# Turning the inverses of the scan's triangles with VectorE's 32x32 transpose and products with an identity instead of through DRAM

## The chip, the cores and the metric

The kernel runs on one core of one Trainium2 chip. The metric is the device time of one execution in microseconds. The kernel before took 2352.26 us, the median of three runs (2348.28 to 2355.29). Smaller is better.

## The reference

The kernel computes one layer of an encoder: a half-step feed-forward network, a mixing layer, a second half-step feed-forward network. Input and output are 1 x 1024 x 1024 float32 (1024 tokens, width 1024).

```python
x = x + 0.5 * post1(FFN1(pre1(x)))
h = pre2(x); z = h @ w_in        # attention q|k|v and RWKV-7 r|k|v|decay|iclr|gate
x = x + post2(concat(attn, rwkv) @ w_out)
x = x + 0.5 * post3(FFN2(pre3(x)))
```

The change touches the RWKV-7 group alone. It has 8 heads of 64 columns and runs over the tokens in both directions. For each direction and head it carries a 64 x 64 state from token to token:

```python
def _rwkv7_step(state, inp):
    r, w, k, v, kk, kka = inp
    sa = jnp.einsum('dbhvk,dbhk->dbhv', state, kk)
    state = state * w[..., None, :] - sa[..., :, None] * kka[..., None, :] + v[..., :, None] * k[..., None, :]
    y = jnp.einsum('dbhvk,dbhk->dbhv', state, r)
    return state, y
```

A token's `sa` needs the state that all tokens before it have left, so the sums inside a chunk of tokens form a system of linear equations with a unit lower triangular matrix, one matrix for each chunk, head and direction.

## The kernel before, in words

**The whole.** The two feed-forward networks (lines L81 and L415 for their products) take the start and the end of the span. Between them come the input projection, the attention, and from about 1180 to 1580 us the stage that this document is about: the scan, the RWKV-7 recurrence, with the output projection of the attention group mixed in as work that fills TensorE's waits.

**The scan.** The 1024 tokens of a direction are cut into 16 chunks of 64, and two chunks make a block, so there are 8 blocks. A chunk has 16 triangles (2 directions, 8 heads) of 64 x 64, a block 32. For each block four functions run:

- `prep(n)` loads the block's inputs (`th_w`, `th_a` and, in one load from `d_rk`, `in`), forms `pr` and `bk` on VectorE and ScalarE, multiplies them on TensorE into `lp` (L836, 32 products of a block), masks `lp` into the triangles `lm` on VectorE (L838), turns the other half of `bk` with `bp` (L844, a transposition through TensorE with an identity), and stores the two diagonal 32 x 32 blocks of every triangle to DRAM (`d_x`, L852).
- `solve(n)` inverts these 64 small triangles. It loads them as `X`, with one triangle on one partition (L862; each is loaded onto two partitions, one of which solves the left 16 columns of the inverse and the other the right 16), and runs 31 steps of forward substitution, two VectorE operations each (L872, L874), on `Ti`. At the end `Ti` has the inverses. VectorE copies a transposed version of them into the free part of `X` (L876). Both are written to DRAM, as `d_t` (L878) and `d_tt` (L879).
- `merge(n)` reads the inverses back from DRAM, now with rows on partitions, as `d` and `tt` (L889, L892), and puts the off-diagonal 32 x 32 block of every 64 x 64 inverse together: 32 products `pa` (L900), two copies by ScalarE (L902), 32 products `pb` (L906), two negations by ScalarE (L908). The result is `tt`, two buffers of which take turns.
- `chain(n)` runs the two chunks, and this is the sequential part. For each chunk: `xu` from the state `sv` (L947), a copy to `xs` by ScalarE (L950), `xu` again as `tt` times `xs` (L958), `uv` by ScalarE (L960), products `st` and `y` (L943), the next state `sv` by VectorE (L974). The values of `v` are loaded into `sv` and `uv` by `values` (L914).

**What sets the order.** The block program (L1262 to L1310) runs `prep` and `solve` of blocks 0 and 1 early, beside the input projection, then `merge(0)` and `prep`, `solve` of block 2, and then for each n: `merge(n)`, `chain(n)`, `prep` and `solve` of block n+3, and one or two tiles of the output projection (48 products `po` each, L1070, after `yat`, `yq`, `yah`, `yal`, whose weights `woh` and `wol` are made from `wor` by L1060). A scheduler decides each engine's order of instructions ahead of time, by priorities and its own estimate of when things are ready; on the chip each engine runs its list in that order and waits where something is not ready. The DMAs of L878, L879, L889, L892 and L914 are issued by GpSimd (POOL), the loads of `prep` and `solve` by SyncE (SP). `X`, `Ti` and their scratch `ttmp` have two buffers, `d` one, and the PSUM tile of `pa` and `pb` one.

Of the kernel before, what the change touches and what calls it, by code (L numbers as in the profile page):

```python
# [163 lines left out]
class _Kernel:  # L164
# [624 lines left out]
    def prep(self, n, p, psum, big):  # L789
# [59 lines left out]
        for par in range(2):  # L849
            for k in range(2):  # L850
                r0 = par * 64 + k * 32
                self.nc.sync.dma_start(_ap(self.x_d[n % 4], (k * 2 + par) * 16 * 1024, [[32, 32], [1024, 16], [1, 32]]),  # L852
                                  lm[r0:r0 + 32, par, :, :, :, k * 32:k * 32 + 32].rearrange("p d i a t -> p (d i a) t"))
        return blk

    def solve(self, n, p):


        nc, V, G = self.nc, self.nc.vector, self.nc.gpsimd
        X = p.tile([128, 32, 32], F32, name="X", tag="X", bufs=2)  # L860
        for q in range(2):
            self.load(X[q * 64:q * 64 + 64].rearrange("p a b -> p (a b)"), self.x_d[n % 4])  # L862
        Ti = p.tile([128, 32, 16], F32, name="Ti", tag="Ti", bufs=2)
        tmp = p.tile([128, 144], F32, name="ttmp", tag="ttmp", bufs=2)
        tf = Ti.rearrange("p a b -> p (a b)")
        G.memset(tf, 0.0)
        for q in range(2):
            G.memset(tf[q * 64:q * 64 + 64, q * 16:512:33], 1.0)
        for s in range(31):
            r, m = 31 - s, s // 2 + 1  # L870
            tv = tmp[:, :r * m].rearrange("p (a b) -> p a b", a=r)
            V.tensor_tensor(tv, X[:, s, s + 1:][:, :, None].to_broadcast([128, r, m]),  # L872
                            Ti[:, s, 0:m][:, None, :].to_broadcast([128, r, m]), op=OP.mult)
            V.tensor_tensor(Ti[:, s + 1:, 0:m], Ti[:, s + 1:, 0:m], tv, op=OP.subtract)  # L874
        Tt = X[:, 0:16, :]
        V.tensor_copy(Tt, Ti.rearrange("p a b -> p b a"))  # L876
        for q in range(2):
            self.nc.gpsimd.dma_start(_ap(self.t_d[n % 4], q * 16, [[1024, 32], [32, 32], [1, 16]]), Ti[q * 64:q * 64 + 32])  # L878
            self.nc.gpsimd.dma_start(_ap(self.tt_d[n % 4], q * 32, [[1024, 64], [64, 16], [1, 32]]), Tt[q * 64:q * 64 + 64])  # L879

    def merge(self, n, blk, p, psum):

        nc, A, T = self.nc, self.nc.scalar, self.nc.tensor
        NI, lm = 2 * BLK * 4, blk["lm"]
        d11 = p.tile([128, NI, 32], F32, name="d11", tag="d11")
        blk["tt"] = tt = self.tt[n % 2]
        for par in range(2):
            o = par * 64
            self.nc.gpsimd.dma_start(d11[o:o + 32], _ap(self.t_d[n % 4], par * 16 * 1024, [[32, 32], [1024, 16], [1, 32]]))  # L889
            for k in range(2):  # L890
                r0 = o + k * 32
                self.nc.gpsimd.dma_start(tt[r0:r0 + 32, :, k * 32:k * 32 + 32],  # L892
                          _ap(self.tt_d[n % 4], (k * 2 + par) * 16 * 1024, [[32, 32], [1024, 16], [1, 32]]))
        pa = psum.tile([128, NI, 32], F32, name="pa", tag="mg")
        am = d11
        lohi = [(slice(o, o + 32), slice(o + 32, o + 64)) for o in (0, 64)]
        for j in range(NI):
            d, i, pr = j // 8, j // 4 % 2, j % 4
            for par, (lo, hi) in enumerate(lohi):
                T.matmul(pa[hi, j, :], lm[lo, par, d, i, pr, 32:64], d11[lo, j, :], start=True, stop=True)  # L900
        for lo, hi in lohi:
            A.copy(am[hi].rearrange("p i (c q) -> p i q c", q=2), pa[hi].rearrange("p i (q c) -> p i q c", q=2))  # L902
        pb = psum.tile([128, NI, 32], F32, name="pb", tag="mg")
        for j in range(NI):
            for lo, hi in lohi:
                T.matmul(pb[lo, j, :], am[hi, j, :], tt[hi, j, 32:64], start=True, stop=True)  # L906
        for lo, hi in lohi:
            A.activation(tt[lo, :, 32:64], pb[lo], AF.Copy, scale=-1.0)  # L908

# [195 lines left out]
    def constants(self):  # L1105
# [6 lines left out]
        for c, t in self.eps.items():  # L1112
# [15 lines left out]
        self.y_d = [self.dram(f"y{d}", [4, 128, S]) for d in range(2)]  # L1128
        self.x_d, self.t_d, self.tt_d = ([self.dram(f"{n}{j}", [r, w]) for j in range(4)]
                                         for n, r, w in (("x", 64, 1024), ("t", 32, 1024), ("tt", 64, 1024)))  # L1130

# [37 lines left out]
    def run(self):  # L1169
# [5 lines left out]
        with self.top as top:  # L1175
# [98 lines left out]
            for n, ct in ((0, 8), (1, 10)):  # L1274
                blk[n] = self.prep(n, sp, pp, (R0, R1)[n])
                self.solve(n, sp)
                self.project_rwkv(zr, pz, x, [(ct, 1), (ct + 1, 1)])
# [13 lines left out]
            def upto(m):  # L1291
                while nxt[0] <= min(m, NB - 1):
                    n = nxt[0]
                    blk[n] = self.prep(n, sp, pp, (R0, R1, B0)[n % 3])
                    self.solve(n, sp)
                    nxt[0] += 1
# [145 lines left out]
```

## Time and profile before

| what | value |
|---|---|
| median of three runs | 2352.26 us (2348.28 to 2355.29) |
| the profiled execution's own time | 2347.61 us |
| its span in the profile | 2345.8 us (1.8 us lie around it) |
| mean granted TensorE clock | 0.962 |
| the scan | about 1180 to 1580 us of the span |
| first and last time that chunk 0 to 15 begin their second `xu` product (L958) | 1299.2 and 1564.3 us |

Times are positions in the span or durations in microseconds. A row of a group gives the line, the engine, the operation, output<-inputs, how many, then the busy time and the mean duration of one in ns, and behind the last bar how long the engine had been idle just ahead of them and who ended it. A row of the timeline gives the start, the length of a run of equal instructions, and in brackets the idle time ahead of it. A float32 product shows as two records on TensorE in these traces (`x64` are 32 products), a transposition through TensorE as one.

### The profile page before, as it was taken

To read this page: it belongs to the slowest core of one execution; us is meant where nothing else is said; L and a number is where in the kernel's file an instruction comes from. 1 tells how busy PE (TensorE), PEld (TensorE's weight loads), DVE (VectorE), ACT (ScalarE), POOL (GpSimd) and SP (SyncE) were. 2 spreads that over 40 slices of the span, in tenths; PEclk is the share of its full clock that TensorE was granted. 3 is DMA by queue.
4 is the path that set the end of the run, shared out by engine and by line. 5 is a ranking of instruction groups with operands and counts; after the bars stand their busy time and mean duration, and the time that the engine had idled before them with its cause. 6 is when DMAs were issued, how large, how long until landed. Compare 5 with 4: busy or idle time off the path is not lost. (4 is left out here: it accounts for less than half of the span.)

```text
span 2345.8 us, 39442 instructions
## 1 busy us (share of the span) xinstructions
PE 2198.8 (94%) x14532; PEld 1776.9 (76%) x14532; DVE 1761.8 (75%) x2869; ACT 1026.5 (44%) x1942; POOL 606.5 (26%) x740
## 2 busy tenths in 40 slices
PE   5999999999999998999996888988699999999997
PEld 4788888878877676788775777766578888887886
DVE  8899999965676244666668777737899999986565
ACT  4333232354567412666544645445443323235453
POOL 6244444410000010111112232332424444441000
PEclk8999999999999998999996898989899999999998
DMA  5344444476671514443269767587435444447665
GB/s 153 99 168 160 172 148 171 160 265 194 197 228 74 218 45 127 117 116 96 60 180 221 192 174 181 136 242 244 157 119 170 161 171 149 171 161 260 191 191 181
DMA packets 360084, 388.13 MB, mean 165 GB/s; under 512 B 74450, under 2 KB 265810, under 8 KB 359892
## 3 DMA queue, kind: packets, MB, share of 16 engines
q1 hardware_dynamic: 309216, 278.53, 39.6%
q0 software_dynamic: 30320, 94.44, 11.4%
q10 hardware_dynamic: 20356, 12.66, 1.8%
q8 instruction: 114, 1.87, 0.3%
q14 instruction: 78, 0.64, 0.1%
HBM read 259.63 MB, written 125.89 MB: 164 GB/s over the span
## 5 line engine op out<-in xcount | busy, mean ns | idle before, releaser
L186 ACT ACTIVATE wh<-raw 128x512 fp32r<-128x512 f32 (+1 forms) x273 | 168.4, 626 | 272.0 <-PE gu L81 96.0
L187 DVE TENSOR_TENSOR wl<-raw,wh 128x512 fp32r<-128x512 f32 (+1 forms) x273 | 275.8, 1013 | 4.1 <-ACT wh L186 3.3
L81 PE MATMUL gu<-xh,wh 128*128 128x512 f32 x704 | 276.9, 394 | 1.1 <-ACT xh L186 1.1
L81 PE MATMUL gu<-xl,wh 128*128 128x512 f32 x704 | 275.9, 392 | 0.0
L81 PE MATMUL gu<-xh,wl 128*128 128x512 f32 x704 | 275.4, 391 | 0.0
L415 PE MATMUL pd<-gl,gwh 128*128 128x512 f32 x616 | 241.2, 392 | 2.9 <-DVE gl L187 2.9
L415 PE MATMUL pd<-gh,gwh 128*128 128x512 f32 x616 | 240.2, 391 | 0.6 <-DVE row L86 0.6
L415 PE MATMUL pd<-gh,gwl 128*128 128x512 f32 x616 | 240.6, 391 | 0.0
L86 DVE TENSOR_TENSOR row<-gu,row 128x512 f32<-128x512 f32 x308 | 206.4, 682 | 25.6 <-PE gu L81 25.2
L187 DVE TENSOR_TENSOR gwl<-graw,gwh 128x512 fp32r<-128x512 f32 (+1 forms) x176 | 116.9, 667 | 127.9 <-ACT gwh L186 125.3
L116 POOL DMA_DIRECT2D d_hid<-row x154 | 84.7, 551 | 471.3 <-DVE row L114 449.2
L186 ACT ACTIVATE gwh<-graw 128x512 fp32r<-128x512 f32 (+1 forms) x176 | 101.4, 576 | 188.6 <-PE pd L415 157.9
L81 PEld LDWEIGHTS gu<-xh,wh 128*128 128x128 f32 x704 | 133.3, 190 | 30.1 <-ACT xh L186 2.8
L81 PEld LDWEIGHTS gu<-xl,wh 128*128 128x128 f32 x704 | 133.2, 189 | 27.5
L81 PEld LDWEIGHTS gu<-xh,wl 128*128 128x128 f32 x704 | 133.1, 189 | 27.6
L415 PEld LDWEIGHTS pd<-gl,gwh 128*128 128x128 f32 x616 | 116.0, 188 | 27.9 <-DVE gl L187 4.1
L415 PEld LDWEIGHTS pd<-gh,gwh 128*128 128x128 f32 x616 | 116.0, 188 | 25.6 <-DVE row L86 0.9
L415 PEld LDWEIGHTS pd<-gh,gwl 128*128 128x128 f32 x616 | 116.1, 188 | 24.1
L187 DVE TENSOR_TENSOR gl<-raw,gh 128x512 fp32r<-128x512 f32 x160 | 112.8, 716 | 18.4 <-ACT gh L186 18.2
L94 ACT ACTIVATE row<-row 128x512 f32<-128x512 f32 x44 | 27.7, 632 | 221.1 <-DVE row L86 213.6
L145 POOL TENSOR_TENSOR ws<-ws 128x512 f32<-128x512 f32 x88 | 114.3, 1299 | 1.2
L186 ACT ACTIVATE gh<-raw 128x512 fp32r<-128x512 f32 x160 | 98.1, 621 | 35.7 <-DMA raw<-in_ffn_w_down_dram 21.7
(351 smaller groups left out, 5292.1 us busy)
## 6 DMA issues: line engine op xcount, KB each, us to landing
d_hid<-row POOLq DMA_DIRECT2D x154, 256.0 KB, 2.4
graw<-d_hid SPq DMA_DIRECT2D x132, 256.0 KB, 3.1
raw<-in_ffn_w_gate_dram SPq DMA_DIRECT2D x88, 256.0 KB, 3.1
raw<-in_ffn_w_up_dram SPq DMA_DIRECT2D x88, 256.0 KB, 3.4
ws<-in_ffn_w_down_dram SPq DMA_DIRECT2D x88, 256.0 KB, 4.5
d_ws<-ws POOLq DMA_DIRECT2D x88, 256.0 KB, 2.4
raw<-d_ws SPq DMA_DIRECT2D x88, 256.0 KB, 2.7
raw<-in_ffn_w_down_dram SPq DMA_DIRECT2D x66, 256.0 KB, 3.5
```

The lines of the kernel that those rows point to most:

```text
L81: self.K.nc.tensor.matmul(ps, a[:, k, :], b[:, k, :], start=(k == 0 and i == 0), stop=(k == 3 and i == 2))
L86: add = lambda o, x: V.tensor_tensor(o, ps, x, op=OP.add)
L94: A.activation(y[:, 0], y[:, 0], AF.Silu)
L116: put = lambda n, y: G.dma_start(self.hid[n - 1, j // 2], y)
L145: G.tensor_tensor(o, a, b, op=OP.subtract)
L186: self.nc.scalar.activation(h, src, AF.Copy)
L187: (eng or self.nc.vector).tensor_tensor(l, src, h, op=OP.subtract)
L415: T.matmul(ps[x], a[:, ts], b, start=(m == 0 and k == 0), stop=(m == NM - 1 and k == 2))
```

## The change

The inverses stay on the chip. `solve(n)` ends with VectorE's transposition of 32 x 32 blocks (L876) where the copy was; its result `D` lies in the first half of `X` and has the inverses with rows on partitions, transposed. What was stored and loaded (`d_t`, `d_tt`: 4 stores and 6 loads for a block) is gone. `merge(n)` makes the transposed form that `chain` needs with 64 products of `D` with an identity (new L889 `pa<-ident,X`), copies it by ScalarE (L890), then does the 32 products of before from `D` (L894), ScalarE's copies (two of L896, one of L897), the other 32 products into the same PSUM tile (L900), and the two negations (L902).

So that the transposition puts things where they belong, the triangles lie in another order in `d_x`, one load instead of two brings `X` in (every row twice, on neighbouring partitions), and the unit diagonals of `Ti` are set from a small constant (`unit`) instead of by a fill. Below the edited lines the program is otherwise the same; `chain`'s lines have moved up by 6 (L947 is now L941, L958 now L952, L943 now L937) and those of the output projection too.

```diff
-                self.nc.sync.dma_start(_ap(self.x_d[n % 4], (k * 2 + par) * 16 * 1024, [[32, 32], [1024, 16], [1, 32]]),
+                self.nc.sync.dma_start(_ap(self.x_d[n % 4], (par * 2 + k) * 16 * 1024, [[32, 32], [1024, 16], [1, 32]]),
...
-        for q in range(2):
-            self.load(X[q * 64:q * 64 + 64].rearrange("p a b -> p (a b)"), self.x_d[n % 4])
+        self.load(X.rearrange("p a b -> p (a b)"),
+                  _ap(self.x_d[n % 4], 0, [[1024, 64], [0, 2], [1, 1024]]))
...
-            G.memset(tf[q * 64:q * 64 + 64, q * 16:512:33], 1.0)
+            G.tensor_copy(tf[:, q * 16:512:33], self.unit[:, q, :])
...
-        Tt = X[:, 0:16, :]
-        V.tensor_copy(Tt, Ti.rearrange("p a b -> p b a"))
-        for q in range(2):
-            self.nc.gpsimd.dma_start(_ap(self.t_d[n % 4], q * 16, [[1024, 32], [32, 32], [1, 16]]), Ti[q * 64:q * 64 + 32])
-            self.nc.gpsimd.dma_start(_ap(self.tt_d[n % 4], q * 32, [[1024, 64], [64, 16], [1, 32]]), Tt[q * 64:q * 64 + 64])
+        D = X[:, 0:16, :]
+        V.transpose(D.rearrange("p j (b q) -> p b j q", q=2), Ti.rearrange("p a b -> p b a"))
+        return D
...
-        d11 = p.tile([128, NI, 32], F32, name="d11", tag="d11")
+        D, am = blk["inv"], p.tile([128, NI, 32], F32, name="am", tag="d11")
         blk["tt"] = tt = self.tt[n % 2]
-        for par in range(2):
-            o = par * 64
-            self.nc.gpsimd.dma_start(d11[o:o + 32], _ap(self.t_d[n % 4], par * 16 * 1024, [[32, 32], [1024, 16], [1, 32]]))
-            for k in range(2):
-                r0 = o + k * 32
-                self.nc.gpsimd.dma_start(tt[r0:r0 + 32, :, k * 32:k * 32 + 32],
-                          _ap(self.tt_d[n % 4], (k * 2 + par) * 16 * 1024, [[32, 32], [1024, 16], [1, 32]]))
         pa = psum.tile([128, NI, 32], F32, name="pa", tag="mg")
-        am = d11
         lohi = [(slice(o, o + 32), slice(o + 32, o + 64)) for o in (0, 64)]
+        for j in range(NI):
+            for r in [r for lo, hi in lohi for r in (hi, lo)]:
+                T.matmul(pa[r, j, :], D[r, j, :], self.ident[r, r], start=True, stop=True)
+        A.copy(tt[:, :, 32:64], pa)
         for j in range(NI):
             d, i, pr = j // 8, j // 4 % 2, j % 4
             for par, (lo, hi) in enumerate(lohi):
-                T.matmul(pa[hi, j, :], lm[lo, par, d, i, pr, 32:64], d11[lo, j, :], start=True, stop=True)
+                T.matmul(pa[hi, j, :], lm[lo, par, d, i, pr, 32:64], D[lo, j, :], start=True, stop=True)
         for lo, hi in lohi:
-            A.copy(am[hi].rearrange("p i (c q) -> p i q c", q=2), pa[hi].rearrange("p i (q c) -> p i q c", q=2))
-        pb = psum.tile([128, NI, 32], F32, name="pb", tag="mg")
+            A.copy(tt[lo, :, 0:32], pa[lo])
+        A.copy(am, pa)
         for j in range(NI):
             for lo, hi in lohi:
-                T.matmul(pb[lo, j, :], am[hi, j, :], tt[hi, j, 32:64], start=True, stop=True)
+                T.matmul(pa[lo, j, :], am[hi, j, :], tt[hi, j, 32:64], start=True, stop=True)
         for lo, hi in lohi:
-            A.activation(tt[lo, :, 32:64], pb[lo], AF.Copy, scale=-1.0)
+            A.activation(tt[lo, :, 32:64], pa[lo], AF.Copy, scale=-1.0)
...
+        self.unit = p.tile([128, 2, 16], F32, name="unit")
+        V, one = self.nc.vector, self.unit[:, 1, 0:1]
+        V.tensor_reduce(out=one, in_=self.ident[:, 1::2], op=OP.add, axis=AX.X)
+        G.tensor_copy(self.unit[:, 1, 1:], one.to_broadcast([128, 15]))
+        G.tensor_scalar(self.unit[:, 0, :], self.unit[:, 1, :], -1.0, 1.0, op0=OP.mult, op1=OP.add)
```

The edit also moves instructions past others, since the scheduler orders them anew. Two places matter below. The first is TensorE at the start of the scan, around the merge of block 0 and the second half of `prep` of block 2. Before:

```order
L836 MATMUL lp<-pr,bk 128x128 x14
L844 MATMUL bp<-ident,bk 128x64 x16
L611 MATMUL vt<-ident,vrev 128x128 x4
L836 MATMUL lp<-pr,bk 128x128 x2
L900 MATMUL pa<-d_12011,lm 32x32
L836 MATMUL lp<-pr,bk 128x128 x14
L844 MATMUL bp<-ident,bk 128x64 x5
L900 MATMUL pa<-d_12011,lm 32x32 x31
L844 MATMUL bp<-ident,bk 128x64 x11
L1081 MATMUL yq<-ident,yat 128x128 x4
L906 MATMUL pb<-tt_11993,d_12011 32x32 x32
```

The same place after the change:

```order
L836 MATMUL lp<-pr,bk 128x128 x2
L889 MATMUL pa<-ident,X 32x32 x64
L836 MATMUL lp<-pr,bk 128x128 x2
L611 MATMUL vt<-ident,vrev 128x128 x4
L836 MATMUL lp<-pr,bk 128x128 x10
L844 MATMUL bp<-ident,bk 128x64 x16
L894 MATMUL pa<-X,lm 32x32 x32
L900 MATMUL pa<-tt_11963,am 32x32 x32
L941 MATMUL xu<-sv,lm 64x64 x16
L1075 MATMUL yq<-ident,yat 128x128 x4
L836 MATMUL lp<-pr,bk 128x128 x16
L844 MATMUL bp<-ident,bk 128x64 x8
```

The whole merge of block 0 and the first `xu` of chunk 0 have moved ahead of the second direction's `lp`, and the 64 new products stand inside the first direction's.

The second place is the first chunk of block 2, on TensorE, which is typical of the blocks in the middle. Before:

```order
L906 MATMUL pb<-tt_11993,d_13399 32x32 x31
L947 MATMUL xu<-sv,lm 64x64 x15
L1081 MATMUL yq<-ident,yat 128x128 x3
L958 MATMUL xu<-xs,tt_11993 64x64 x16
L943 MATMUL st<-uv,bt 64x64
L943 MATMUL y<-lm,uv 64x64
L1070 MATMUL po<-woh,yah 128x512
```

After the change, where the products with an identity are already those of block 3:

```order
L900 MATMUL pa<-tt_11963,am 32x32 x32
L941 MATMUL xu<-sv,lm 64x64 x8
L889 MATMUL pa<-ident,X 32x32 x15
L952 MATMUL xu<-xs,tt_11963 64x64 x16
L889 MATMUL pa<-ident,X 32x32 x33
L937 MATMUL st<-uv,bt 64x64
L937 MATMUL y<-lm,uv 64x64
L889 MATMUL pa<-ident,X 32x32 x5
L1064 MATMUL po<-woh,yah 128x512
```

Of block 3's 64 new products 53 have come to stand in this chunk, 15 of them ahead of its second `xu` and 33 behind it. They need VectorE's transposition of block 3. Its end on VectorE, before, from the last masking L838 of that stretch on (`bk` and `th_a` belong to `prep` of the next block; the rest is `solve(3)`):

```order
L838 TENSOR_TENSOR lm<-lp,k_tri 128x512
L872 TENSOR_TENSOR ttmp<-X,Ti 128x91
L820 TENSOR_SCALAR bk<-th_a,in_13692 128x8x64
L874 TENSOR_TENSOR Ti<-Ti,ttmp 128x7x13
L821 TENSOR_SCALAR bk<-bk,th_w 128x8x64
L872 TENSOR_TENSOR ttmp<-X,Ti 128x78
L874 TENSOR_TENSOR Ti<-Ti,ttmp 128x6x13
L872 TENSOR_TENSOR ttmp<-X,Ti 128x70
L874 TENSOR_TENSOR Ti<-Ti,ttmp 128x5x14
L872 TENSOR_TENSOR ttmp<-X,Ti 128x56
L874 TENSOR_TENSOR Ti<-Ti,ttmp 128x4x14
L872 TENSOR_TENSOR ttmp<-X,Ti 128x45
```

Five more rows of the substitution, down to 128x16, stand between these and the copy L876. After, down to the transposition:

```order
L838 TENSOR_TENSOR lm<-lp,k_tri 128x512
L872 TENSOR_TENSOR ttmp<-X,Ti 128x30
L820 TENSOR_SCALAR bk<-th_a,in_13824 128x8x64
L874 TENSOR_TENSOR Ti<-Ti,ttmp 128x2x15
L821 TENSOR_SCALAR bk<-bk,th_w 128x8x64
L872 TENSOR_TENSOR ttmp<-X,Ti 128x16
L874 TENSOR_TENSOR Ti<-Ti,ttmp 128x16
L876 STREAM_TRANSPOSE X<-Ti 128x16x16x2
```

Before, 14 operations of the substitution stand behind that masking; after, 4 do. The other 10, `ttmp` of 128x91 to 128x45 with their subtractions, have moved ahead of it.

Over all 8 blocks, the 64 products of block 0 stand inside `prep` of block 2, those of block 1 among `po`. Of the 384 of blocks 2 to 7, 150 have come to stand inside the waits of a chunk for `xs` or `uv` (22, 53, 21, 28 and 26 in blocks 2 to 6), the others between other products.

More of the change, by code (lines that the diff above doesn't have):

```diff
@@ L1128, in constants @@
         self.y_d = [self.dram(f"y{d}", [4, 128, S]) for d in range(2)]
-        self.x_d, self.t_d, self.tt_d = ([self.dram(f"{n}{j}", [r, w]) for j in range(4)]
-                                         for n, r, w in (("x", 64, 1024), ("t", 32, 1024), ("tt", 64, 1024)))
+        self.x_d = [self.dram(f"x{j}", [64, 1024]) for j in range(4)]
     def mix_columns(self):
@@ L1294, in upto @@
                     blk[n] = self.prep(n, sp, pp, (R0, R1, B0)[n % 3])
-                    self.solve(n, sp)
+                    blk[n]["inv"] = self.solve(n, sp)
                     nxt[0] += 1
```

2 lines of the change are left out of this document (1 added, 1 removed).

## The prediction, made before the changed kernel was run

> **What bounds the kernel now.** I read the page's first two parts, then the scan by stages, then what the removed lines waited for.
>
> ```profile
> PE 2198.8 (94%) x14532; PEld 1776.9 (76%) x14532; DVE 1761.8 (75%) x2869; ACT 1026.5 (44%) x1942; POOL 606.5 (26%) x740
> PEclk8999999999999998999996898989899999999998
> ```
>
> TensorE (PE) is busy for 94% of the span, so work that is added to it is paid for unless it falls into one of its gaps. The second row is its clock in 40 slices of 58.6 us; the only slice below 8 (a 6) lies at the start of the scan, from about 1230 us. The scan by stages (PE's busy time, its clock and the DMA share are what I use):
>
> ```profile
> core 0: us, PE busy (x) PEld busy (x) DVE busy (x) ACT busy (x) POOL busy (x), PEclk, DMA share, GB/s
> 1180.00:1255.00 75.00, 63.42 (x401) 50.42 (x399) 54.74 (x128) 39.80 (x83) 2.89 (x8) 0.95 0.79 204
> 1255.00:1305.00 50.00, 30.56 (x348) 25.75 (x349) 36.94 (x108) 25.09 (x43) 22.91 (x38) 0.52 0.88 211
> 1305.00:1340.00 35.00, 33.61 (x540) 27.44 (x538) 30.46 (x87) 21.80 (x41) 4.67 (x8) 1.00 0.72 188
> 1340.00:1380.00 40.00, 35.28 (x639) 29.07 (x637) 32.57 (x97) 22.48 (x43) 15.17 (x25) 0.96 0.72 188
> 1380.00:1420.00 40.00, 33.52 (x592) 27.96 (x592) 27.93 (x79) 20.38 (x39) 11.27 (x20) 0.95 0.72 179
> 1420.00:1460.00 40.00, 36.93 (x555) 29.33 (x553) 31.50 (x95) 17.34 (x33) 12.05 (x21) 0.84 0.74 186
> 1460.00:1500.00 40.00, 38.10 (x522) 31.06 (x523) 32.07 (x94) 19.37 (x37) 11.92 (x20) 0.87 0.51 129
> 1500.00:1540.00 40.00, 37.54 (x850) 31.47 (x848) 23.92 (x78) 18.05 (x34) 21.08 (x32) 1.00 0.50 126
> 1540.00:1580.00 40.00, 34.39 (x507) 26.72 (x506) 11.29 (x22) 18.47 (x34) 11.57 (x12) 0.74 0.98 298
> ```
>
> There are three different stages. At the start (1255 to 1305) PE stands idle for 50 - 30.56 = 19.4 us and runs at half clock. In the middle (1340 to 1500) it is idle for 4.7 + 6.5 + 3.1 + 1.9 = 16.2 us in 160: it is nearly the bound, and what is left are short waits of the chain. At the end there are 5.6 us in 40.
>
> **What the change removes.** First the trip through DRAM. These are groups (POOL's waits) and the DMA's own rows (KB each, us from issue to landing):
>
> ```profile
> L878 POOL DMA_DIRECT2D d_t<-Ti x16 | 12.9, 803 | 73.9 <-DVE Ti L874 44.9 <-DMA X<-d_x 24.3 <-issue 4.7
> ```
>
> ```profile
> q0 software_dynamic: 6464, 16.79, 17.9%
> d_t<-Ti POOLq DMA_DIRECT2D x16, 64.0 KB, 4.2
> d_tt<-X POOLq DMA_DIRECT2D x16, 128.0 KB, 4.8
> d<-d_t POOLq DMA_DIRECT2D x16, 64.0 KB, 3.6
> tt<-d_tt POOLq DMA_DIRECT2D x32, 64.0 KB, 3.4
> ```
>
> Store and load take 4.8 + 3.4 = 8.2 us one behind the other. Whether that is on the path shows in block 3, where its inverses are ready and where they are used:
>
> ```profile
> 1373.29 0.68 DVE L838 TENSOR_TENSOR lm<-lp,k_tri 128x512 f32<-128x512 f32 x1
> ...
> 1375.43 0.23 DVE L872 TENSOR_TENSOR ttmp<-X,Ti 128x78 f32<-128x78 f32 x1
> ...
> 1377.49 0.19 DVE L872 TENSOR_TENSOR ttmp<-X,Ti 128x30 f32<-128x30 f32 x1
> ...
> 1378.36 0.60 DVE L876 COPY X<-Ti 128x512 f32<-128x512 f32 x1
> ```
>
> ```profile
> 1376.14 0.55 PE L1081 MATMUL yq<-ident,yat 128*128 128x128 f32 x3
> 1377.66 1.15 PE L958 MATMUL xu<-xs,tt 64*64 64x64 f32 x32 [0.97 <-ACT xs L950]
> 1379.91 0.33 PE L943 MATMUL st<-uv,bt 128*64 128x64 f32 x2 [1.10 <-ACT uv L960]
> ```
>
> ```profile
> 1402.51 1.20 PE L900 MATMUL pa<-d,lm 32*32 32x32 f32 x64
> ```
>
> The copy ends at 1378.96 and the first product with it starts at 1402.51, 23.5 us later. Of those the trip fills 8.2. So in the middle it is **hidden anyway**, and its end gives nothing directly. What it gives indirectly is transport: 16 x 64 + 16 x 128 + 16 x 64 + 32 x 64 KB = 6.3 MB of the 16.79 on POOL's queue. One wait in the scan could profit:
>
> ```profile
> DVE pr L816 <- DMA in<-d_rk: 7.9, 6, 2.1
> ```
>
> VectorE waits 7.9 us in 6 times for `in`, at a DMA share of 0.72. If a quarter of that goes, it is **-2 us** (between 0 and -4). POOL issues less, and as it is busy for 11 to 15 us in 40 here, its new copies onto the diagonals cost nothing.
>
> **What it adds.** The 64 products with an identity are 128 records a block. The nearest row is the one of 1402.51, the same 32x32 float32 products: 64 records in 1.20 us, 18.75 ns each, so **2.4 us a block**. Blocks 2 to 7, which lie in the middle, get 6 x 2.4 = 14.4 us. The scheduler has put 150 of their 384 products into the waits for `xs` and `uv`, which the rows above show as 0.97 and 1.10 us: 300 x 18.75 ns = 5.6 us hidden. The others stand between other products and are paid for: 14.4 - 5.6 = 8.8 us. Block 1's stand among `po` at 1305 to 1340, where PE is idle for only 1.4 us in 35, so their 2.4 us are paid as well: **+11.2 us** together (bounds: 0, if they fill the 16.2 idle microseconds of the middle, and 16.8 with nothing hidden).
>
> A rule of the Trainium skill bears on this price: "TensorE: Matmul & The Clock Gate", section "Wait — 56ns, not 53.3ns?", says that consecutive products never start less than about 25 ns apart, however small they are. By it the 128 records would be an estimated 3.2 us a block, and the sum some 5.6 us higher over blocks 1 to 7. This trace's 18.75 ns differs, and decides. Another speaks against this form of the change: "Perfetto Trace Analysis", section "Transposes", asks for logical transpositions to use the transpose form instead of a standard product. `bp` (L844) does that, with one record each; the estimate by it would be 64 records and 1.2 us less a block, which this change leaves lying.
>
> The transposition by VectorE takes the place of a copy of the same tile. No row shows one. The rows for the two ends are the copy (0.60 us, above) and VectorE's slow reciprocal, with the reciprocal 8 times as long for 512 columns as for 64:
>
> ```profile
> L902 ACT COPY d<-pa 32x512 f32<-32x512 f32 x16 | 9.8, 614 | 0.6 <-PE pa L900 0.3
> L908 ACT ACTIVATE tt<-pb 32x512 f32<-32x512 f32 x16 | 9.4, 586 | 3.6 <-PE pb L906 3.4
> L217 DVE RECIPROCAL rs<-rs 128x64 f32<-128x64 f32 x1 | 0.5, 546 | 0.0
> ```
>
> So it is between 0.60 and 8 x 0.546 = 4.4 us; I take 0.60, since both read a strided tile and write one of 512 columns, and it costs nothing more then. At 4.4, it would come 3.8 us late in each block, which is the first rival below in a worse form.
>
> ScalarE goes from 4 to 6 operations in a merge at about 0.6 us each (rows above). It is busy for half of the time, so only the part between two products counts: three instead of two between `pa` and `pb`, and one new one ahead of `pa`. Other products stand there in most blocks; blocks 2, 4 and 6 have the least of them, and I count one operation of 0.6 us in each: **+2 us** (0 to 4).
>
> **The start.** Here merge 0 moves ahead of the second `lp`. The rows are of PE and ScalarE:
>
> ```profile
> 1278.10 0.80 PE L836 MATMUL lp<-pr,bk 64*128 64x128 f32 x4 [11.13 <-DVE bk L828]
> ...
> 1284.30 1.91 PE L900 MATMUL pa<-d,lm 32*32 32x32 f32 x62
> ...
> 1292.28 1.92 PE L906 MATMUL pb<-tt,d 32*32 32x32 f32 x64 [3.99 <-issue]
> ...
> 1299.19 1.12 PE L958 MATMUL xu<-xs,tt 64*64 64x64 f32 x16 [3.09 <-ACT xs L950]
> ```
>
> ```profile
> 1288.40 0.72 ACT L1060 ACTIVATE woh<-wor,c_attn_out_g 128x512 fp32r<-128x512 f32 x1 [8.15 <-DMA wor<-in_w_out_dram]
> ...
> 1293.30 1.87 ACT L934 COPY lm<-pr 64x512 f32<-64x512 f32 x3
> ...
> 1298.56 0.58 ACT L950 COPY xs<-xu 128x512 f32<-128x512 f32 x1
> ```
>
> `pa`, `pb` and their gaps go into the hole of 11.13 us. That would free the 7.8 us of 1.91, 1.92 and 3.99, but `xs` can't come before what stands ahead of it on ScalarE: the third `woh`, whose weights land at 1288.40, then three copies `lm` and itself, 1288.40 + 0.72 + 1.87 + 0.58 = 1291.6, 7.6 us before the present 1299.19. Against it, the 64 new products stand ahead of the hole at half clock: 62 records in 1.91 us are 30.8 ns each, so 3.9 us for 128, which delay the first direction's `lp`, its masking and what VectorE does next. Between -7.6 and +3.9 I take **-4 us**, because the hole is nearly three times as long as the delay. The page "TensorE: Matmul & The Clock Gate", section "What's actually happening", has the clock go to half after an idle window of some 3.4 us; the 0.52 of this stage agrees, and if the moved products shorten the hole, the half clock may end sooner.
>
> **The end.** Merge 7 stands between the last state and the last block's first product:
>
> ```profile
> 1539.68 0.61 PE L943 MATMUL st<-sv,ident 64*64 64x256 f32 x2 [0.64 <-DVE sv L974]
> ...
> 1549.81 1.19 ACT L908 ACTIVATE tt<-pb 32x512 f32<-32x512 f32 x2 [3.03 <-PE pb L906]
> ...
> 1552.75 1.98 PE L958 MATMUL xu<-xs,tt 64*64 64x64 f32 x32
> ```
>
> 13.1 us pass from the state to that product. Without the trip `pa` could begin earlier, but the order keeps other work in there, and more of ScalarE's copies. **-1 us**, between -7 (the merge's half of it gone) and +4 (the identity products exposed there too, with one more copy).
>
> **The sum:** -2 + 11.2 + 2 - 4 - 1 = +6.2. On the profiled execution's 2347.61 that is 2353.8. The median of the runs is 4.65 us above that execution, so the time to be measured is **2358 us**.
>
> **The rivals.** *Slower: TensorE waits for the solve.* In the middle the 23.5 us between the inverse and its first use were a buffer; now 15 of block 3's products (30 records, 0.56 us) stand in order ahead of the second `xu`, at 1377.66, and need the transposition. Had it still ended at 1378.96, that `xu` would start at 1379.52, 1.9 us late, and 6 such blocks give 11.2 us: 2358 + 11 = **2369**. It decides if VectorE doesn't get the 10 moved operations done ahead of the masking. Eight of them take from 1375.43 to 1377.49, 0.26 us each, so ten take 2.6; the transposition then ends at 1376.4, and the 15 products are through by 1376.9. For the rival speaks that only 0.7 us are left; against it, that VectorE had 7.4 us of idle time in 1340 to 1380.
>
> *Faster: the start closes.* All of -7.6 there, -4 by the transport, the tail half won (-4), and the added products filling more of the waits (+5 instead of +11.2) with +2 on ScalarE: -8.6, thus 2339 on the profiled execution and **2344**. For it speaks the 19.4 idle microseconds in 50 at half clock; against it, that `woh` and `in` still arrive when they do.
>
> *The change does only what it adds:* the trip was hidden, and nothing at the start, at the end or in transport is won. 11.2 + 2 = +13.2: **2365**. It is on the slower side.
>
> **How the numbers follow.** The forecast has 0.50: it is within 0.3% (7 us, which is about what a measurement of this kernel can tell from no change) with 0.30, slower (above 2359.3) with 0.17 and faster (below 2345.2) with 0.03. The waits for the solve have 0.14 and the pure addition 0.12, both slower, 0.02 of each within. The faster rival has 0.24, of which 0.02 falls within. Together: faster 0.25, same 0.36, slower 0.39. The range goes from 2338 (the faster rival with the tail's -7 and ScalarE's part hidden, rounded down) to 2375 (the waits for the solve with the 5.6 hidden microseconds exposed).
>
> **What will show it.** Right is the forecast if the identity products take about 2.4 us a block at full clock, if in the middle a block takes some 2 us longer than now, and if the first chunk's `xu` starts around 1295. Rows of idle time at L889 that are put down to the transposition on VectorE show the first rival, and a transposition well over 0.6 us too. An `xu` of chunk 0 before 1292 with a clock above 0.7 in 1255 to 1305 shows the second. It is wrong in kind if a stage outside of 1180 to 1580 changes by more than a microsecond or two.

## The result, and the profile after

The changed kernel is **faster**, by a little but clear of noise: 2343.27 us, the median of 12 runs (2338.73 to 2353.74), against 2353.79 for the kernel before in 12 runs beside it. The ratio is 0.9962 (0.9946 to 0.9979), 9 us less. Forecast were 2358 us and a time between 2338 and 2375. So the time lies inside the range and on the other side of no change. It is the number of the rival "the start closes" (2344), but that is luck: that rival had 7.6 us won at the start and 5 us paid for the products, and the runs below give 4 for the start (e1) and 17 to 24 for the products (e8, e16).

In what follows a ratio is always to the runs of the kernel before on the same chip beside it, with its 95% interval; 0.001 is 2.35 us. One profiled execution may lie several microseconds from its kernel's median (that of before took 2347.61), so ratios say how much, and profiles where. The two executions that are compared here lie only 4.5 us apart, and 3.8 of that are there before the first merge: the L876 that ends block 0's inverse starts that much earlier, first before, then after.

```profile
1259.12 0.60 DVE L876 COPY X<-Ti 128x512 f32<-128x512 f32 x1
```

```profile
1255.29 1.05 DVE L876 STREAM_TRANSPOSE X<-Ti 128x512 f32<-128x512 f32 x1
```

The last product of the input projection (L510) begins at 1250.92 before and at 1247.09 after. In the other executions it lies anywhere from 1244.4 (e6) to 1254.0 (e7), so the shift can't safely be put down to the change. Where it says "without the shift" below, the 3.8 us are taken off.

The page's first two parts, after:

```profile
PE 2206.1 (94%) x15556; PEld 1783.6 (76%) x15556; DVE 1768.5 (76%) x2870; ACT 1031.8 (44%) x1958; POOL 551.5 (24%) x662
PEclk8999999999999999999997999989899999999999
```

TensorE has 1024 records more and is busy 7.3 us longer. The slice at the start of the scan that had a 6 for the clock has a 7 now, and it is still the lowest. The stages, with the same bounds as before:

```profile
core 0: us, PE busy (x) PEld busy (x) DVE busy (x) ACT busy (x) POOL busy (x), PEclk, DMA share, GB/s
1255.00:1305.00 50.00, 38.30 (x684) 33.29 (x683) 38.45 (x107) 28.12 (x51) 12.89 (x23) 0.68 0.76 200
1305.00:1340.00 35.00, 31.65 (x555) 25.22 (x554) 30.83 (x95) 20.43 (x38) 2.74 (x7) 0.95 0.66 188
1340.00:1380.00 40.00, 35.90 (x806) 30.73 (x801) 29.23 (x80) 21.20 (x41) 5.61 (x11) 0.90 0.58 160
1380.00:1420.00 40.00, 37.04 (x738) 30.99 (x736) 32.70 (x92) 22.54 (x44) 6.81 (x13) 0.97 0.55 156
1420.00:1460.00 40.00, 32.91 (x626) 27.66 (x624) 30.77 (x90) 20.11 (x38) 5.28 (x9) 0.88 0.57 157
1460.00:1500.00 40.00, 38.54 (x707) 31.65 (x707) 32.20 (x100) 18.38 (x35) 4.75 (x8) 0.99 0.42 115
```

At the start TensorE is idle for 11.7 us instead of 19.4, and its clock is 0.68 instead of 0.52. In the middle the DMA share falls from between 0.72 and 0.74 to between 0.55 and 0.58 (0.51 to 0.42 in the last row). TensorE's idle time there is 15.6 us (16.2 before), although 8.3 us of new products (L889 in these four stretches) were put in.

The start, on TensorE and ScalarE (the same places as in the prediction):

```profile
1256.83 1.93 PE L889 MATMUL pa<-ident,X 32*32 32x32 f32 x128
...
1266.28 1.85 PE L894 MATMUL pa<-X,lm 32*32 32x32 f32 x64 [2.72 <-ACT tt L890]
1270.09 1.92 PE L900 MATMUL pa<-tt,am 32*32 32x32 f32 x64 [1.95 <-ACT am L897]
1271.93 2.37 PE L941 MATMUL xu<-sv,lm 64*64 64x64 f32 x32
1278.24 1.11 PE L1075 MATMUL yq<-ident,yat 128*128 128x128 f32 x4 [3.94 <-DVE yat L1072]
1281.25 4.26 PE L836 MATMUL lp<-pr,bk 64*128 64x128 f32 x29 [1.89 <-DVE bk L828]
...
1286.13 0.47 PE L952 MATMUL xu<-xs,tt 64*64 64x64 f32 x2
```

```profile
1278.03 0.72 ACT L1054 ACTIVATE woh<-wor,c_attn_out_g 128x512 fp32r<-128x512 f32 x1 [3.10 <-DMA wor<-in_w_out_dram]
1278.78 1.87 ACT L928 COPY lm<-pr 64x512 f32<-64x512 f32 x3
1280.67 0.58 ACT L944 COPY xs<-xu 128x512 f32<-128x512 f32 x1
```

The second `xu` of chunk 0 begins at 1286.13, 13.1 us earlier, or 9.3 without the shift. In place of one hole of 11.13 us ahead of the second `lp`, the merge now runs there, between waits of 2.72, 1.95, 3.94 and 1.89 us. The third `woh` comes at 1278.03, not at 1288.40: its weights arrive 10.4 us sooner. Of these 3.8 are the shift. Another 2.9 are an earlier issue: `wor` has two buffers, and the third load goes out when VectorE's `wol` has read the first of them. These are the rows of both, before:

```profile
1278.07 0.74 DVE L1061 SCALAR_TENSOR_TENSOR wol<-wor,c_attn_out_g,woh 128x512 fp32r<-128x512 f32 x1
1278.84 1.75 SPq L182 DMA_DIRECT2D wor<-in_w_out_dram  x2
```

After:

```profile
1271.31 0.74 DVE L1055 SCALAR_TENSOR_TENSOR wol<-wor,c_attn_out_g,woh 128x512 fp32r<-128x512 f32 x1
1272.08 0.34 SPq L182 DMA_DIRECT2D wor<-in_w_out_dram  x1
```

The last 3.6 us are a shorter time under way: 6.0 us from issue to use instead of 9.6. What surrounded it is seen on POOL, first before, then after:

```profile
1268.79 0.53 POOL L866 MEMSET Ti<- 128x512 f32 x1 [5.52 <-DMA d_t<-Ti]
...
1271.52 0.68 POOL L889 DMA_DIRECT2D d<-d_t  x1
...
1278.48 1.78 POOL L914 DMA_DIRECT2D sv<-d_vt  x3 [0.41 <-DMA tt<-d_tt]
```

```profile
1262.48 1.25 POOL L908 DMA_DIRECT2D uv<-d_vt  x2 [3.27 <-DMA d_vt<-vts]
1263.72 2.38 POOL L908 DMA_DIRECT2D sv<-d_vt  x4
```

Before, the loads of `v` for the first chunks stood behind the trip's loads and went out at 1275 to 1281, together with the next block's `in` and the weights. These are what was issued from 1276 to 1290 before, with the time to landing:

```profile
in<-d_rk SPq DMA_DIRECT2D x1, 768.0 KB, 8.7
...
wor<-in_w_out_dram SPq DMA_DIRECT2D x2, 256.0 KB, 9.5
...
th_a<-d_a SPq DMA_DIRECT2D x1, 256.0 KB, 10.6
```

After, they go out at 1262 to 1267, 9 us sooner without the shift. Some 4 us of that come from the order, not from the trip's place in the queue: these loads need the stores of `v` (`d_vt`), and the last four of those were issued from 1265.75 on before and from 1257.95 on after, since the new order on TensorE has `vt` ahead of most of `lp` and `bp` (the first place under "The change"). From chunk 2 on little is left: it begins at 1335.5 instead of 1341.0, chunk 15 at 1558.0 instead of 1564.3, which is 1.7 and 2.5 us without the shift.

### The profile page after: what moved, and what is told of

It reads as the page before. It is cut to its first block, busy times and chain, and to the rows that moved or that the text cites. A ratio compares the mean times of both kernels' runs of the same rounds, so it can differ in the third digit from the quotient of the medians.

```text
span 2341.3 us, 41376 instructions
## 1 busy us (share of the span) xinstructions
PE 2206.1 (94%) x15556; PEld 1783.6 (76%) x15556; DVE 1768.5 (76%) x2870; ACT 1031.8 (44%) x1958; POOL 551.5 (24%) x662
```

## The experiments

All changes are to the changed kernel or to the one before, as said. The hybrids do some blocks in the new form and the others through DRAM, by a set of block numbers.

| run | what | ratio to before | interval |
|---|---|---|---|
| | the changed kernel | 0.9962 | 0.9946 to 0.9979 |
| e5 | the changed kernel again | 0.9965 | 0.9944 to 0.9986 |
| e1 | block 0 alone changed | 0.9982 | 0.9965 to 0.9998 |
| e2 | blocks 1 to 7 alone changed | 1.0003 | 0.9988 to 1.0019 |
| e3 | changed, transfers put back in all blocks | 1.0013 | 0.9996 to 1.0031 |
| e6 | the same in block 0 alone | 0.9991 | 0.9971 to 1.001 |
| e17 | the same in blocks 1 to 7 alone | 0.9983 | 0.9966 to 1.0 |
| e4 | changed, products with the identity doubled | 1.0076 | 1.0052 to 1.0099 |
| e8 | changed, second transposition on VectorE instead of the products | 0.9891 | 0.9864 to 0.9917 |
| e16 | e8 again | 0.9863 | 0.9843 to 0.9883 |
| e9 | e8 with 64 unused products a block | 0.9933 | 0.9906 to 0.996 |
| e10 | e8 with the transfers put back | 0.9926 | 0.9897 to 0.9955 |
| e13 | block 0 alone as in e8 | 0.9993 | 0.9981 to 1.0005 |
| e14 | blocks 1 to 6 alone as in e8 | 0.9945 | 0.9924 to 0.9966 |
| e15 | block 7 alone as in e8 | 0.9981 | 0.9966 to 0.9997 |
| e7 | before, first `v` loads by SyncE | 0.9955 | 0.9939 to 0.9972 |
| e11 | changed, first `v` loads by SyncE | 0.996 | 0.9942 to 0.9979 |
| e12 | e8, first `v` loads by SyncE | 0.992 | 0.9889 to 0.9951 |
| e18 | before, all `v` loads by SyncE | 1.0001 | 0.9982 to 1.0019 |

Each edit makes the scheduler order the engines anew. In the traces, e5 has the changed kernel's order on every engine and e17 on TensorE, VectorE and ScalarE, and e16 has that of e8. In the other runs the order differs from that of the kernel they are compared with, and its part of a difference is not known.

My first theory was that the gain comes from the start (block 0), the rivals that it is the transport in every block, or TensorE's clock.

**Which blocks, with the products (e1, e2, and e5 as control).**

```diff
+        if n not in NEW:
+            return self.solve_old(n, p)
...
+        if n not in NEW:
+            return self.merge_old(n, blk, p, psum)
```

> Block 0 alone goes the new way (transposition on VectorE, products with an identity); blocks 1 to 7 go through DRAM as before. The order on TensorE at the start is that of the changed kernel, in the middle that of before. Theory 'start' (the gain comes from block 0's merge, which no longer waits for the trip through DRAM in the hole of 11 us, and the other seven blocks come out even): 5 to 10 us faster than before, and chunk 0's second xu begins near 1286 us instead of 1299. Theory 'transport' (the gain is the traffic that is gone in every block): an eighth of it, 1 us. Theory 'clock' (the added products keep TensorE's clock up): 0 to 2 us.

> Blocks 1 to 7 go the new way, block 0 through DRAM as before. Start: no faster than before, 0 to 10 us slower, since the added products of seven blocks (16.8 us, part of them hidden) are paid and nothing is won at the start. Transport: 7 to 9 us faster. Clock: 6 to 9 us faster, with a granted clock of the middle near 0.95 and above.

> The changed kernel once more (all 8 blocks the new way, same order of instructions on every engine), beside the runs below on one chip. Expected as measured: 9 us faster than before (5 to 13).

Measured: -4 us for block 0 alone, +1 us for the seven others, -8 us for all again. That fits the theory "start", if a little below its 5 to 10 us, and speaks against "clock" and against "transport" as stated, unless in the seven blocks a gain and the price of the products cancel. e14 below fits that.

**The transfers put back (e3, e6, e17).** The stores and loads of before, of the same shapes, into dead parts of `Ti` and `X`. No computation reads their data, but GpSimd's fill of `Ti` for a later block has to wait until the dead loads have landed.

```diff
+            G.dma_start(_ap(self.t_d[n % 4], q * 16, [[1024, 32], [32, 32], [1, 16]]), Ti[q * 64:q * 64 + 32])
+            G.dma_start(_ap(self.tt_d[n % 4], q * 32, [[1024, 64], [64, 16], [1, 32]]), D[q * 64:q * 64 + 64])
...
+            self.nc.gpsimd.dma_start(dd[o:o + 32].rearrange("p (j t) -> p j t", t=32), _ap(self.t_d[n % 4], par * 16 * 1024, [[32, 32], [1024, 16], [1, 32]]))
+            for k in range(2):
+                r0 = o + k * 32
+                self.nc.gpsimd.dma_start(dt[r0:r0 + 32], _ap(self.tt_d[n % 4], (k * 2 + par) * 16 * 1024, [[32, 32], [1024, 16], [1, 32]]))
```

> The changed kernel with the transfers of before added again in all 8 blocks (4 stores and 6 loads a block, same shapes, on the same queue), into dead tiles that no computation reads. Transport: back to the time of before, 9 us above the changed kernel, or slower. Start: the merge no longer waits for them, so at most 3 us are lost and it stays 5 us or more faster than before. Clock: like the changed kernel.

> The changed kernel with the transfers of before added again in block 0 alone, into dead tiles. Theory 'start, transport' (the trip's 10 transfers of block 0 hold back, on GpSimd's queue and in the transfer engines, the loads of v and of the weights that the first chunk needs): most of what all eight cost comes back, so 6 to 12 us above the changed kernel, and chunk 0's second xu begins near 1294 us. Rival 'transport everywhere': an eighth, 1 to 2 us above the changed kernel.

> The changed kernel with the transfers of before added again in blocks 1 to 7 alone, into dead tiles; every engine but GpSimd keeps the changed kernel's order. If the transfers are what the middle's gain is made of: 6 us or more above the changed kernel (its 9 us of gain mostly gone). By the prediction's 2 us of transport: within 3 us of the changed kernel.

Measured, against the changed kernel's 0.9965 (e5): +11 us in all blocks (5 to 18, the two intervals combined), +6 in block 0 alone (-1 to 13), +4 in the seven others (-2 to 11). The first is clear, its two parts each only likely; they add up to it. So with the transfers back the gain of 9 us is gone, although no computation needs them. Transport is not all that came back, though. At the start of e3:

```profile
1276.69 0.53 POOL L866 MEMSET Ti<- 128x512 f32 x1 [4.35 <-DMA Ti<-d_t]
```

```profile
1285.92 2.12 PE L953 MATMUL xu<-sv,lm 64*64 64x64 f32 x32
```

```profile
1292.10 1.33 ACT L1066 ACTIVATE woh<-wor,c_attn_out_g 128x512 fp32r<-128x512 f32 x2 [5.48 <-DMA wor<-in_w_out_dram]
1293.34 0.56 ACT L956 COPY xs<-xu 128x512 f32<-128x512 f32 x1
```

`xs` comes at 1293.34, 13 us later than in the changed kernel (2.3 of it were there at block 0's transposition), although the merge (its last product ends at 1275.9) is done long before. The loads of `v` again go out at 1277 to 1282, behind the dead loads and a fill that waits 4.35 us for one of them. But the order is another one as well: in e3 and in e6 the first `xu` stands behind the second direction's `lp` and `bp`, where the changed kernel has it ahead of them (1271.93), and `xs` stands behind two more `woh`, which the changed kernel does at 1288.79, 8 us after its `xs`. So the late start of e3 is not the merge's own wait, but how much of it is transport and how much order is not shown. e17 is the cleanest, since it keeps the order (the fill of `Ti` waits there too, 5.2 us in all), and its 4 us (-2 to 11) are not clear of noise.

**The price of the products (e4, e8, e9, e16).** In e4 every product with the identity is done twice. e8 replaces them by a second transposition of VectorE's, from `D` into `tt`:

```diff
-        for j in range(NI):
-            for r in [r for lo, hi in lohi for r in (hi, lo)]:
-                T.matmul(pa[r, j, :], D[r, j, :], self.ident[r, r], start=True, stop=True)
-        A.copy(tt[:, :, 32:64], pa)
+        self.nc.vector.transpose(tt[:, :, 32:64], D)
...
-            A.copy(tt[lo, :, 0:32], pa[lo])
-        A.copy(am, pa)
+            A.copy(tt[lo, :, 0:32], tt[lo, :, 32:64])
+        for lo, hi in lohi:
+            A.copy(am[hi], pa[hi])
```

e9 is e8 plus 64 products of `ident` with itself ahead of `pa`:

```diff
+        for j in range(NI):
+            for lo, hi in lohi * 2:
+                T.matmul(pa[hi, j, :], self.ident[lo, lo], self.ident[lo, lo], start=True, stop=True)
```

> Every product with an identity is done twice, 64 more a block, 19.2 us more of TensorE at 18.75 ns a record, 16.8 of them outside of block 0. By the prediction's step on their price, two thirds are exposed: 11 us above the changed kernel, thus 2 us slower than before. If the gaps take them all (part of theory start too): under 4 us above the changed kernel. Clock: no slower than the changed kernel, perhaps faster.

> The changed kernel without the products with an identity: VectorE transposes the 32x32 blocks of D a second time, straight into tt (1.06 us each by the changed kernel's rows), so TensorE loses 128 records a block, 19.2 us at 18.75 ns. By the prediction's step (two thirds of the products exposed): 8 to 12 us faster than the changed kernel. By the accounting of the middle (from chunk 2 to 15 the added products lengthened it by 1 or 2 us at most): within 4 us of the changed kernel.

> The kernel with the second transposition on VectorE, plus 64 products of an identity with itself in every merge, whose results are overwritten: the 19.2 us of TensorE's time that the changed kernel's products cost, without their wait for VectorE and without the copy behind them. If their price is TensorE's time alone: 15 to 20 us slower than the second transposition (5 to 11 us faster than before, like the changed kernel). If it is the wait and the longer chain of the merge: within 6 us of the second transposition.

> All blocks in that form, again, beside the three parts on the same chip: 20 to 30 us faster than before, as e8. If the parts add up, e13, e14 and e15 together give this.

Measured: the second helping costs 26 us (19 to 33) over e5, more than the 19.2 us that I had expected of its records, of which the trace shows 12.9 (both helpings are busy for 29.5 us, the changed kernel's for 16.6). Without the products the kernel is 17 us (9 to 25) faster than e5, in e16 even 24. The bare time of 64 products, without their wait, is 10 us (1 to 19) of that against e8 and 16 against e16. So the products with their wait cost about what I had expected for all of their records, 19.2 us, and bare ones half of that or more. That is about the prediction's 11.2 us or more; whether the waits hid a third of them, these intervals don't tell. The groups of the changed kernel, and of e8:

```profile
L889 PE MATMUL pa<-ident,X 32*32 32x32 f32 x1024 | 16.6, 208 | 5.6 <-issue 3.7 <-ACT tt L902 2.0
...
L876 DVE STREAM_TRANSPOSE X<-Ti 128x512 f32<-128x512 f32 x8 | 8.4, 1056 | 0.3
```

```profile
L893 ACT COPY tt<-tt 32x512 f32<-32x512 f32 x16 | 9.8, 613 | 11.9 <-DVE tt L887 11.7
...
L876 DVE STREAM_TRANSPOSE X<-Ti 128x512 f32<-128x512 f32 x8 | 8.4, 1056 | 0.2
L887 DVE STREAM_TRANSPOSE tt<-X 128x512 f32<-128x512 f32 x8 | 5.7, 709 | 0.1
```

VectorE's second transposition takes 709 ns where TensorE needs 16.6 / 8 = 2.1 us of its busy time a block. ScalarE's copy waits for it, 11.7 us in all; what that costs, no run tells. A page of the Trainium skill has this rule ("VectorE: DVE Perf Modes", section "Rules for kernel authors"): for blocks of 32x32 within a bank VectorE's transposition is the fastest way. These runs agree, with 17 to 24 us.

**The transfers without the products (e10).** The edits of e8 and e3 together.

> The kernel with the second transposition, with the transfers of before added again in all 8 blocks, into dead tiles. If the transfers cost the same 12 us as they do in the changed kernel: 12 to 15 us faster than before. If they were only costly because TensorE was loaded with the products: within 5 us of the second transposition, 20 us or more faster than before.

Measured: 17 us faster than before, 8 us (-1 to 17) slower than e8, which is not quite clear of noise. The transfers cost about as much as in the changed kernel, with the order changed here too.

**Which blocks, without the products (e13, e14, e15).** The hybrid with the form of e8.

> Block 0 alone in the form with two transpositions on VectorE, without products; blocks 1 to 7 through DRAM as before. If the start holds the rest of the gain: 12 us or more faster than before. If it is spread: 4 to 7 us faster, as block 0 with products was.

> Blocks 1 to 6 alone in that form; blocks 0 and 7 through DRAM. By the prediction the trip is hidden in the middle, by 23.5 us of slack, and only its transport is won: 0 to 4 us faster than before. If the middle holds the rest: 10 us or more faster.

> Block 7 alone in that form; blocks 0 to 6 through DRAM. By the prediction's bounds the end is worth between 7 us faster and 4 us slower, taken as 1 us faster. If the end holds the rest, as the profile of e10 suggests (from chunk 12 to 15 it took 27.1 us instead of 36.8): 5 to 10 us faster.

Measured: block 0 alone -2 us (-4 to +1), blocks 1 to 6 alone -13 us (-18 to -8), block 7 alone -4 us (-8 to -1). Without products against it, most of the gain is in the middle, where I had the trip hidden, and the theory "start" falls as the whole answer. The three add up to -19 us, all blocks together give -26 and -32. Between 7 (not clear of noise) and 13 us come only when all are done; no run tells why. The profiled execution of e14 can't say where its 13 us are won, since it was the slowest of its six (2345.89 against a median of 2336.49).

**GpSimd's queue (e7, e11, e12, e18).** In the kernel before, the trip stays and the loads of `v` go to SyncE, for the first two chunks (e7) or all (e18); e11 and e12 do e7's edit on the changed kernel and on e8.

```diff
-            self.nc.gpsimd.dma_start(t[o:o + 64, :, par].rearrange("p d a c -> p d (a c)"),
+            (self.nc.sync if ch < 2 else self.nc.gpsimd).dma_start(t[o:o + 64, :, par].rearrange("p d a c -> p d (a c)"),
```

> The kernel before, the trip through DRAM left as it is, but the loads of v for the first two chunks are issued by SyncE instead of standing behind the trip's loads on GpSimd's queue. Theory 'queue' (it is their place in the queue that held back the start): 3 to 8 us faster than before, with xs of chunk 0 no longer waiting for a weight load that takes 9 us. Theory 'bytes' (the trip's short runs themselves fill the transfer engines): within 2 us of before.

> The changed kernel with the loads of v for the first two chunks issued by SyncE, which made the kernel before 11 us faster. If that gain came from getting these loads from behind the trip's on GpSimd's queue, there is nothing left to gain here: within 4 us of the changed kernel. If it came from something else (the order of SyncE's loads, or the order after the scan): about 10 us faster than the changed kernel, 19 us faster than before.

> The second transposition on VectorE and the loads of v for the first two chunks on SyncE together, as a candidate for the fastest. If the queue's relief is already in the change: within 4 us of the second transposition alone (25 us faster than before). If it is a gain of its own: 30 us or more faster than before.

> The kernel before with all loads of v on SyncE instead of GpSimd, in all 16 chunks; the trip stays. If the place of these loads behind the trip on GpSimd's queue costs time in the middle too: 15 us or more faster than before, more than the 11 us of the first two chunks. If it costs time at the start alone: about 11 us. If SyncE's queue, which also has the loads of prep, is now the one that is in the way: less than that.

Measured: e7 is 11 us faster than before, as much as the whole change; on the changed kernel the same edit adds nothing (e11, -1 us against e5), on e8 it loses 7 (-3 to 16), and with all loads on SyncE nothing is left (e18). e7 and e11 fit the view that the change freed these loads. In e7's profile the third `wor` load has half of them and the second `in` behind it instead of beside it, and it takes 2.8 us instead of 9.5. But block 0's trip gone from the queue gave only 4 us (e1) and 2 us (e13), so e7's 11 us are not explained by the queue alone. Its order on TensorE differs as well (24 of the 48 products `po` that stood ahead of chunk 2 come later). This stays open.

## Why the prediction was wrong

**The step that failed** is in the part on what the change removes: "in the middle it is hidden anyway, and its end gives nothing directly", with "-2 us" for transport as all that was left. In parts, the sum had -4 for block 0 and +10.2 for the other seven (-2 + 11.2 + 2 - 1). Measured are -4 (-8 to 0, e1) and +1 (-3 to 4, e2), so the error lies in blocks 1 to 7. (The 5 us that all eight blocks give beyond these two are not clear of noise.) There the trip's end is worth far more: blocks 1 to 6 alone become 13 us (8 to 18) faster when nothing is put in its place on TensorE (e14), where the prediction had -2. In all 8 blocks it is 26 to 32 us (e8, e16), where the terms for transport, start and end give 7. The 23.5 us between the inverse and its first use showed that the *data* had time. They said nothing of what ten transfers a block do to the others, nor of the order that the scheduler finds without them. I took the price of transport from one row, VectorE's wait for `in`, and a quarter of it. With the transfers put back, and the order they bring, 11 us (e3) and 8 us (e10) are lost.

- **Transport, -2 (0 to -4):** mis-sized as the whole of what the middle wins. Transport alone, with the order kept, is 4 (-2 to 11) in blocks 1 to 7 (e17), which doesn't contradict the bounds; in all 8 blocks, with the order changed too, it is 8 to 11.
- **The start, -4 (-7.6 to +3.9):** right in size by e1, -4. By the profile chunk 0 comes 9.3 us earlier without the shift and chunk 2 1.7. The floor of 1291.6 fell, since it took the landing of `wor` at 1288.40 as fixed. That load came 10.4 us sooner: 3.8 by the shift, 2.9 because the buffer it waited for was read sooner, 3.6 by a shorter time under way. The same slip is in the case against the faster rival ("`woh` and `in` still arrive when they do").
- **The end, -1 (-7 to +4):** -4 (-8 to -1) for block 7 alone, without products (e15). Mis-sized inside its bounds.
- **The products, +11.2 (0 to 16.8):** right in kind, perhaps too small: 17 (9 to 25) with their wait by e8, 24 by e16, and 10 (1 to 19) bare by e9, in all 8 blocks. A record took 15 ns at the start (128 in 1.93 us), below the 18.75 that I used. The 25 ns of the Trainium skill's "TensorE: Matmul & The Clock Gate", section "Wait — 56ns, not 53.3ns?", don't hold here for a record; a product, which is two records, took 30.
- **The transposition, 0.60 (to 4.4):** 1.056 us, 0.46 more than the copy, 3.6 us of VectorE over 8 blocks. Of TensorE's idle time at L889 only 0.2 us are put down to VectorE.
- **TensorE waiting for the solve, the slower rival:** it did not happen. In block 2's first chunk the new products ahead of `xu` waited for the PSUM tile, not for VectorE:

```profile
1370.24 1.07 DVE L876 STREAM_TRANSPOSE X<-Ti 128x512 f32<-128x512 f32 x1
```

```profile
1372.73 0.64 PE L889 MATMUL pa<-ident,X 32*32 32x32 f32 x30 [1.42 <-ACT tt L902]
1373.35 1.97 PE L952 MATMUL xu<-xs,tt 64*64 64x64 f32 x32
```

The transposition ends at 1371.31, 5 us ahead of the 1376.4 that I had worked out (`xu` itself is 4.3 us earlier, of which 3.8 are the shift). That step was right.

Of its signs, the price of the products held (2.1 us a block where it said 2.4). A block in the middle is not 2 us longer, as it said: from chunk 2 to 15 it takes 222.5 us, before it took 223.3. The first chunk's `xu` comes ahead of the faster rival's 1292 (1289.9 without the shift), but with a clock of 0.68, below that rival's 0.7.

What stays open: how the middle's 13 us (e14) come about. Putting the transfers back in blocks 1 to 7 takes only about 4 (-2 to 11) of the changed kernel's gain (e17). The rest may be the order that the scheduler finds when a merge no longer waits for the trip, or TensorE's clock. From chunk 2 to 15 the clock of the profiled executions is 0.89 before, 0.93 in the changed kernel and 0.92 in e1, where the middle is as before, so it changes between executions as well. Over all runs it does differ: the mean granted clock is 0.968 in e5 against 0.960 in the kernel before beside it, 0.968 against 0.960 in e8, 0.967 against 0.961 in e14, but only 0.963 against 0.961 in e1, e13 and e15. Among the 29 runs of the kernel before that stood beside e5, 0.001 more clock goes with some 1.6 us less, so by this estimate a rise of 0.006 to 0.008 would be 9 to 12 us, about the size of the middle's gain. It is not sufficient, since e3 has 0.966 against 0.961 and is no faster, and whether the clock is a cause of the shorter time or a sign of fewer gaps is not shown.

## What to carry to other kernels

Time between a result and its first use shows that a trip is hidden for its own data; to price the trip, add up which transfers stand behind it in its queue and which run beside it, and how much longer than elsewhere these take. In this case even that leaves most of the middle's gain unexplained, so trying it on a part of the blocks is the surer price. A time at which a load lands is no floor for a forecast if the change moves what the load waits for, here the use of its buffer, or takes away what it was competing with. Before two profiles are compared by position, look how far apart they are ahead of the first changed instruction. Where TensorE is nearly the bound, as here, a block transposition is better on an engine with room: the same edit with two transpositions on VectorE gives 26 to 32 us instead of 9.

## What the hardware showed that I had not expected

- At the start of the scan a 256 KB load of `wor` took 9.5 us, with the DMA share at 0.88; some 12 us later two loads of the same kind took 3.2.
- VectorE's transposition of a 128x512 float32 tile took 1056 ns reading `Ti` with a stride and 709 ns reading `D` in order.
- Of two equal helpings of small products the second made TensorE busy for 12.9 us more and cost 26 us (19 to 33): what was added to a nearly full TensorE cost more than its own time, with the new order of the other engines in it.
